# Decoder layer: the instruction order from a list scheduler with deadlines worked back from the matmuls, and the residual update on VectorE alone

## The chip, the cores and the metric

One core of a Trainium2 chip. The metric is the device time of one execution in microseconds; the kernel before took 1973.88 us (median of 3 runs, 1972.43 to 1973.93).

## What is computed

One layer of a decoder for 256 tokens and a width of 2048, in f32, with an RMS norm before and after each of four sub-layers:

```python
h = h + 0.5 * rmsnorm(swiglu(rmsnorm(h), ...))        # ff1: 2048 -> 2 x 5632 -> 2048
h = h + rmsnorm(mix(rmsnorm(h)))                       # one input projection; sparse attention (8 heads)
                                                       # beside a gated linear recurrence; one output projection
h = h + 0.5 * rmsnorm(swiglu(rmsnorm(h), ...))        # ff2
h = h + rmsnorm((p @ w_ple_proj) * sigmoid(rmsnorm(h) @ w_ple_gate))   # ple
```

## The kernel before, in words

**Matmuls.** Weights come as *items* of 256 x 512 (512 KB). There are 692 of them: ff1 264, mix 128, ff2 264, ple 36. An item is loaded by SP into one of four `raw` tiles, and split into a high and a low part in one of eight `ring` slots: ACT makes the high part, DVE the low part ("ring split" below means DVE's half; with a gain it is a SCALAR_TENSOR_TENSOR of 128x512, two per item). An item is then multiplied with both blocks of 128 tokens (tb = 0 and 1), six matmuls of 128x512 per block. Block 1 follows block 0 at a lag of 4 or 5 items (`LAG`). A group of items adds up in one PSUM bank: A_76, A_77, A_78, B_79, B_80, B_81; the banks T_82 and T_83 serve transposes and small matmuls. The moving operand is a ring slot, the stationary one a slice of `uT` (input of a phase, transposed, high and low), `hT` (hidden units of a feed-forward phase) or `oT`.

**Inside a feed-forward phase.** A chunk of 512 hidden units is a gate group (A) and an up group (B). ACT takes silu of the gate into `sg`, DVE multiplies it with the up group into `hid`, PE transposes hid in four pieces (`tr`), and ACT and DVE split the result into hT. The down-projection's groups (`ev_down`) are added into `y`, 512 columns at a time (c = 0 to 3).

**Between phases.** `after_y` squares y with a running sum on ACT and multiplies y by the gain `gpost` on POOL (into `tmp` for c = 3). At c = 3, `finish` makes the block's statistic (sum on DVE, root on ACT, reciprocal on DVE), and `new_h` updates the residual h for the four c. For c = 0 and 1 that is one instruction of DVE; for c = 2 and 3 it is two of POOL. Then `next_u` transposes each piece of h on PE and splits it into uT, ACT the high and DVE the low part. `square_u` squares h for the next phase's first norm. There are three such boundaries: ff1 to mix, mix to ff2, ff2 to ple. At the end of ple all four pieces are on DVE, and h goes out by SP.

**What sets the order.** Every engine runs its instructions in the order in which the program issues them. `Emitter` keeps a clock of its own: `charge_pe` moves it by a fixed cost per matmul, `charge` estimates when ACT, DVE and POOL finish. Work beside the stream is put in a heap with a time (`after`: estimated readiness plus a slack of 500 or 800 ns; `later`: a fixed delay) and issued when the clock has passed it. `run_ops` walks through the matmuls and emits splits up to 10 us (`LOOK`) ahead of it, and loads as far as the raw tiles allow. `Engine.__getattr__` is the helper through which every operation of ACT, DVE, POOL and PE goes (line 176, so nearly all rows have that line); it issues at once. Loads of the gains (`load_gpost`) and of h stand where the program calls them. Tables of ACT are loaded early at four places by hand.

Of the kernel before, what the change touches and what calls it, by code (L numbers as in the profile page):

```python
# [153 lines left out]

def _free(ap):
    n = 1
    for d in ap.shape[1:]:
        n *= d
    return n


class Engine:
# [4 lines left out]
    def __init__(self, em, key, engine):  # L167
        self.em, self.key, self.engine = em, key, engine

    def __getattr__(self, name):  # L170
        f = getattr(self.engine, name)
        if name == "dma_start":
            return f

        def call(out, *args, **kw):
            r = f(out, *args, **kw)  # L176
# [7 lines left out]
            else:  # L184
                n = max([_free(out)] + [_free(a) for a in args[:1] if hasattr(a, "shape")])
# [8 lines left out]
            return r  # L194
# [3 lines left out]
def _build(nc, tc, ctx, dr, out):  # L198
    em = Emitter()
    sy = nc.sync  # L200
    ac, ve, gp_, pe = (Engine(em, k, e) for k, e in (("A", nc.scalar), ("V", nc.vector), ("G", nc.gpsimd), ("P", nc.tensor)))
# [237 lines left out]
    def finish(phase_next, tb, half):  # L439

        rstd(st[:, SS + tb * 4:SS + tb * 4 + 4], 4, col(RPOST + tb), half)
        if phase_next is None:
            if tb == 0:
                nc.scalar.preload_act_table(AF.Sigmoid)
            for c in range(4):
                new_h(tb, c, True)
                sy.dma_start(out[tb, :, c * 512:(c + 1) * 512], h[:, tb, c * 512:(c + 1) * 512])
        else:
# [7 lines left out]
            ready = em.ready, em.last  # L456
            for c in range(4):
                em.ready, em.last = ready
# [5 lines left out]
    def after_y(tb, c, phase_next, half, gain):  # L464
# [8 lines left out]
        gp_.tensor_tensor(tmp[:, tb] if c == 3 else y[:, tb, cc], y[:, tb, cc], gpost[:, cc], ALU.mult)  # L473
        if c == 3:
            finish(phase_next, tb, half)

# [7 lines left out]
    def open_pool(name, old=None):  # L484
        if old is not None:
            pools.pop(old).close()
# [14 lines left out]
    def ffn(ph, phase_next, get):  # L501
# [21 lines left out]
        def ev_down(half, oc):  # L523
            def f(tb, ps):
# [3 lines left out]
                else:  # L528
                    if oc == 2 and tb == 0:
                        nc.scalar.preload_act_table(AF.Sqrt)  # L530
# [506 lines left out]
    def ple(get):  # L1037
# [8 lines left out]
        def ev_gate(c):  # L1046
            def f(tb, ps):
                sg = get("sg")[:, tb]
                ac.activation(sg, ps, AF.Sigmoid, scale=col(RPRE + tb))
                if c == 3:  # L1050
                    nc.scalar.preload_act_table(AF.Sqrt)
# [49 lines left out]
    nc.scalar.preload_act_table(AF.Silu)  # L1101
# [116 lines left out]
    em.drain()  # L1218
    for s in list(pools.values()):
# [56 lines left out]
```

## Time and profile before

| | |
|---|---|
| median of 3 runs | 1973.88 us |
| the profiled execution: its own time | 1972.35 us |
| its span, first to last instruction | 1970.5 us |
| mean granted TensorE clock | 0.996 |
| bytes moved | 372.86 MB, mean 189 GB/s |

Times in rows are us from the span's start. PE is TensorE's matmul, PEld its weight load, DVE VectorE, ACT ScalarE, POOL GpSimd, SP SyncE, which issues the DMAs. A row names the tile written, `<-`, and the tiles read, and then the shapes. In a list by time, what stands in brackets at the end of a row is how long the engine had been idle before, and what ended that. A clock of 1.00 is full speed; PE has the levels 1.2 and 2.4 GHz. "x4" behind a row is a count of like instructions in a row.

### The profile page before, as it was taken

The page shows a single profiled execution, that of the slowest core. Times are in us where ns is not written, and L with a number is a line of the kernel's source. Part 1 is how long each engine was busy: PE and PEld are TensorE (multiplying, and loading weights), DVE is VectorE, ACT ScalarE, POOL GpSimd, SP SyncE. Part 2 cuts the span into 40 slices and gives each one's busy share as a digit, 9 for nine tenths or more (in the row PEclk, how much of TensorE's full clock was granted, in tenths as well). Part 3 has the DMA queues.
Part 4 walks back from the last instruction along what each step waited for, and adds up shares of the span by engine and source line. Part 5 has one row for each costly group of instructions (what it writes and reads, how often), then busy time and mean ns, then how long its engine had stood idle before and what let it go on. Part 6 is the DMA issues. An engine that isn't in the chain of part 4 may idle for free.

```text
span 1970.5 us, 24737 instructions
## 1 busy us (share of the span) xinstructions
PE 1941.5 (99%) x8896; PEld 1605.3 (81%) x8896; DVE 1143.8 (58%) x1597; ACT 1112.4 (56%) x1707; POOL 188.2 (10%) x225
## 2 busy tenths in 40 slices
PE   9999999999999999999999899999999999999998
PEld 7888888888888887888888688888888888888776
DVE  6655554455555557766767755555444555554665
ACT  7655544455554446766797665555444555544564
POOL 3000010000000013103511400000000000000301
PEclk9999999999999999999999999999999999999999
DMA  8755565565565655762446455555555556556463
GB/s 285 267 182 184 179 199 191 190 197 191 186 192 185 190 171 178 251 225 73 154 160 222 150 199 195 189 192 183 191 192 193 191 183 196 188 185 195 157 221 118
DMA packets 107850, 372.86 MB, mean 189 GB/s; under 512 B 11856, under 2 KB 19024, under 8 KB 106960
## 3 DMA queue, kind: packets, MB, share of 16 engines
q1 hardware_dynamic: 107584, 371.19, 57.5%
q8 instruction: 69, 1.13, 0.2%
q14 instruction: 53, 0.43, 0.1%
q10 hardware_dynamic: 144, 0.11, 0.0%
HBM read 369.15 MB, written 2.10 MB: 188 GB/s over the span
## 4 chain that ended last, share of the span: by engine, by line
PE 93%; DVE 3%; ACT 1%; issue 1%; DMA 0%; POOL 0%; SPq 0%; DVEq 0%; ACTq 0%; POOLq 0%
PE A L176 63%; PE B L176 29%; PE T L176 2%; DVE ring L176 2%; DVE uT L176 0%; DVE y L176 0%; ACT junk L176 0%; DVE h L176 0%; ACT ring L176 0%; ACT y L176 0%; DMA raw<-ff_w_gate 0%; POOL rt L176 0%; DVE st L176 0%; ACT st L176 0%; DVE sm L176 0%
## 5 line engine op out<-in xcount | busy, mean ns | idle before, releaser
L176 DVE SCALAR_TENSOR_TENSOR ring<-raw,vec,ring 128x512 fp32r<-128x512 f32 (+3 forms) x992 | 716.8, 765 | 388.1 <-ACT ring L176 386.2
L176 PE MATMUL A<-ring,uT 128*128 128x512 f32 (+3 forms) x3552 | 859.6, 389 | 9.4 <-DVE ring L176 3.5
L176 ACT ACTIVATE ring<-raw,vec 128x512 fp32r<-128x512 f32 (+3 forms) x992 | 669.8, 713 | 297.2 <-PE A L176 151.4
L176 PEld LDWEIGHTS A<-ring,uT 128*128 128x128 f32 x3552 | 654.1, 188 | 143.7 <-DVE ring L176 6.7
L176 PE MATMUL B<-ring,uT 128*128 128x512 f32 x2208 | 541.2, 389 | 0.0
L176 PE MATMUL A<-ring,hT 128*128 128x512 f32 x2112 | 490.6, 392 | 0.0
L176 PEld LDWEIGHTS B<-ring,uT 128*128 128x128 f32 x2208 | 414.1, 188 | 86.2
L176 PEld LDWEIGHTS A<-ring,hT 128*128 128x128 f32 x2112 | 396.2, 188 | 86.2
L176 DVE TENSOR_TENSOR ring<-raw,ring 128x1024 fp32r<-128x1024 f32 x196 | 242.7, 1241 | 255.7 <-ACT ring L176 255.6
L176 ACT ACTIVATE ring<-raw 128x1024 fp32r<-128x1024 f32 x196 | 207.3, 1058 | 240.1 <-PE A L176 190.0
L176 POOL TENSOR_TENSOR y<-y,gpost 128x512 f32<-128x512 f32 x24 | 31.1, 1297 | 1277.2 <-ACT junk L176 1277.2
L176 ACT ACTIVATE hT<-T 128x512 fp32r<-128x512 f32 x44 | 26.2, 598 | 95.9 <-PE T L176 95.9
L176 ACT ACTIVATE sg<-A,st 128x512 f32<-128x512 f32 x52 | 35.8, 688 | 72.7 <-PE A L176 72.6
L176 DVE TENSOR_TENSOR hT<-T,hT 128x512 fp32r<-128x512 f32 x44 | 30.3, 691 | 73.1 <-ACT hT L176 72.6
L176 ACT ACTIVATE junk<-y 128x512 f32<-128x512 f32 x31 | 19.6, 632 | 58.0 <-DVE y L176 58.0
L176 DVE SCALAR_TENSOR_TENSOR hid<-B,st,sg 128x512 f32<-128x512 f32 x44 | 32.8, 748 | 23.8 <-PE B L176 23.8
L176 PE MATMUL B<-ring,oT 128*64 128x256 f32 (+1 forms) x224 | 42.0, 327 | 0.0
L176 PEld LDWEIGHTS B<-ring,oT 128*64 128x64 f32 (+1 forms) x224 | 33.4, 157 | 5.4
L176 POOL TENSOR_TENSOR per_sc<-per_sc 128x32 f32<-128x32 f32 (+1 forms) x24 | 9.3, 388 | 193.9 <-ACT per_sc L176 188.9
L176 PEld LDWEIGHTS T<-cst,hid 128*128 128x128 f32 x176 | 21.9, 140 | 5.6
L176 PE MATMUL T<-cst,hid 128*128 128x128 f32 x176 | 26.2, 272 | 0.0
L176 ACT ACT_TABLE_LOAD x20 | 25.7, 1283 | 0.4
(157 smaller groups left out, 671.7 us busy)
## 6 DMA issues: line engine op xcount, KB each, us to landing
raw<-ff_w_up SPq DMA_DIRECT2D x176, 512.0 KB, 4.2
raw<-ff_w_down SPq DMA_DIRECT2D x176, 512.0 KB, 3.3
raw<-ff_w_gate SPq DMA_DIRECT2D x175, 512.0 KB, 4.1
raw<-w_out SPq DMA_DIRECT2D x32, 512.0 KB, 4.4
raw<-w_ple_gate SPq DMA_DIRECT2D x32, 512.0 KB, 4.3
raw<-cmp_w SPq DMA_DIRECT2D x16, 512.0 KB, 4.6
raw<-w_in_q SPq DMA_DIRECT2D x16, 512.0 KB, 4.6
raw<-w_in_y SPq DMA_DIRECT2D x16, 512.0 KB, 4.3
```

The costliest lines, as they stand in the source:

```text
L176: r = f(out, *args, **kw)
```

## The change

Every operation, and every DMA of SP, now goes into a list (`Plan.add`) with the blocks of memory that it reads and writes, and estimates of how long it holds its engine (`step`) and when its result is there (`lat`). `Plan.flush` (called when a pool of tiles is opened, three times, and at the end) finds the dependences, gives each matmul a due time by its place in the stream (transposes and small matmuls 2 us earlier, `AUX`), works due times back through the dependences, and then places the operations one at a time: the engine that can start first takes, of what is ready, what is due first. A load isn't placed more than 15 us ahead of its due time (`AHEAD`). DVE and POOL exclude each other in it where both use the port (`port`). In the order of the planned starts, the operations are then issued. Table loads are put ahead of the first operation of a new set (`SETS`), in place of the four by hand.

Beside that, `new_h` is one instruction of DVE for every c, and the multiplication by gpost for c = 3 is DVE's too. The Emitter's heap stays and sets the order in which the list is recorded.

```diff
+class Plan:
...
+    HOP, SAME, PE_MARGIN, NEAR, AUX, AHEAD = 60.0, 35.0, 150.0, 120.0, 2000.0, 15000.0
...
+            if name == "scalar_tensor_tensor":
+                s = 132.0 + 1.04 * n
+            elif name in ("tensor_scalar", "tensor_copy") and len(sbuf) == 1:
+                s = 135.0 + 0.53 * n
+            else:
+                s = 65.0 + 1.045 * n
...
+            two = len(sbuf) >= 2 or name in ("tensor_scalar", "tensor_copy")
+            return s, s + 85.0, two and n > 32
...
+    def flush(self):
...
+        t = max(self.nominal, self.free["P"])
+        for o in ops:
+            if o["key"] == "P":
+                o["due"] = t - (self.AUX if o["aux"] else 0.0)
+                t += o["step"]
+            else:
+                o["due"] = None
+        self.nominal = t
+        for i in range(len(ops) - 1, -1, -1):
+            o = ops[i]
+            due = o["due"] if o["due"] is not None else t
+            for j in o["succ"]:
+                q = ops[j]
+                raw = q["deps"][i]
+                if q["key"] == o["key"]:
+                    d = o["lat"] + self.SAME if raw and o["key"] in "AVG" else o["step"]
+                else:
+                    d = o["lat"] + self.HOP
+                if o["key"] == "S":
+                    d = 2300.0 + o["bytes"] / 250.0
+                due = min(due, q["due"] - d)
+            o["due"] = due
+
+        left = [len(o["deps"]) for o in ops]
...
+        at = [max(o["floor"], o["due"] - self.AHEAD if o["key"] == "S" else 0.0) for o in ops]
...
+        while len(order) < n:
+            best = None
+            for k, c in ready.items():
+                if not c:
+                    continue
+                f = self.free[k]
+                t0 = min(max(f, at[i]) for i in c)
+                if best is None or t0 < best[0]:
+                    best = (t0, k)
+            t0, k = best
+            c = ready[k]
+            i = min((i for i in c if at[i] <= t0 + self.NEAR), key=lambda i: (ops[i]["due"], i))
+            c.remove(i)
+            o = ops[i]
+            s = max(t0, at[i])
+            if o["port"]:
+                s = max(s, self.port["G" if k == "V" else "V"])
+                self.port[k] = s + o["lat"] - 30.0
+            start[i] = o["start"] = s
+            self.free[k] = s + o["step"]
+            end = s + o["lat"]
+            if k == "S":
+                self.dma = max(s + 2000.0, self.dma) + o["bytes"] / 310.0
+                end = self.dma + 300.0
+            order.append(i)
+            o["end"] = end
...
+            for j in o["succ"]:
+                q = ops[j]
+                raw = q["deps"][i]
+                if q["key"] == k and k != "S":
+                    r = end + self.SAME if raw and k in "AVG" else s + 1.0
+                else:
+                    r = end + self.HOP + (self.PE_MARGIN if q["aux"] else 0.0)
+                at[j] = max(at[j], r)
+                left[j] -= 1
+                if not left[j]:
+                    ready[q["key"]].append(j)
+        for i in sorted(range(n), key=lambda i: (start[i], i)):
+            ops[i]["fn"]() if ops[i]["fn"] else ops[i]["load"]["preload"]()
...
         def call(out, *args, **kw):
-            r = f(out, *args, **kw)
+            n = max([_free(out)] + [_free(a) for a in args[:1] if hasattr(a, "shape")])
+            self.plan.add(self.key, name, lambda: f(out, *args, **kw), out, args, kw, n)
+            if name == "activation":
+                func = args[1]
+                self.plan.ops[-1]["preload"] = lambda: self.engine.preload_act_table(func)
+            if self.key == "S":
+                return
...
-    def new_h(tb, c, last=False):
+    def new_h(tb, c):
         cc = slice(c * 512, (c + 1) * 512)
         a, hh = tmp[:, tb] if c == 3 else y[:, tb, cc], h[:, tb, cc]
-        if c < 2 or last:
-            ve.scalar_tensor_tensor(hh, a, col(RPOST + tb), hh, op0=ALU.mult, op1=ALU.add)
-        else:
-            gp_.tensor_scalar(a, a, col(RPOST + tb), None, op0=ALU.mult)
-            gp_.tensor_tensor(hh, a, hh, ALU.add)
+        ve.scalar_tensor_tensor(hh, a, col(RPOST + tb), hh, op0=ALU.mult, op1=ALU.add)
 
...
         if phase_next is None:
-            if tb == 0:
-                nc.scalar.preload_act_table(AF.Sigmoid)
             for c in range(4):
-                new_h(tb, c, True)
+                new_h(tb, c)
                 sy.dma_start(out[tb, :, c * 512:(c + 1) * 512], h[:, tb, c * 512:(c + 1) * 512])
...
         else:
             ac.activation(junk, y[:, tb, cc], AF.Square, accum_out=col(SS + tb * 4 + c))
-        gp_.tensor_tensor(tmp[:, tb] if c == 3 else y[:, tb, cc], y[:, tb, cc], gpost[:, cc], ALU.mult)
         if c == 3:
+            ready = em.ready, em.last
+            ve.tensor_tensor(tmp[:, tb], y[:, tb, cc], gpost[:, cc], ALU.mult)
+            em.ready, em.last = ready
             finish(phase_next, tb, half)
+        else:
+            gp_.tensor_tensor(y[:, tb, cc], y[:, tb, cc], gpost[:, cc], ALU.mult)
...
     def open_pool(name, old=None):
+        plan.flush()
```

What the new order does at three places (of each program the rows as they stand, the older one first). `h` is the residual, `y` and `tmp` the output of a phase, `st` the statistic, `ring<-raw,vec,ring` a ring split.

**PE, boundary ff1 to mix.** Transposes of h (`<-cst,h`) stand among the last matmuls of ff1 (`hT`) and the first of mix (`uT`).

```order
L176 MATMUL A_77<-ring,hT 128x512 x24
L176 MATMUL T_83<-cst,h 128x128 x4
L176 MATMUL T_82<-cst,h 128x128 x4
L176 MATMUL A_77<-ring,hT 128x512 x12
L176 MATMUL B_79<-cst,h 128x128 x4
L176 MATMUL A_78<-ring,uT 128x512 x12
L176 MATMUL B_81<-cst,h 128x128 x4
L176 MATMUL A_78<-ring,uT 128x512 x6
L176 MATMUL T_83<-cst,h 128x128 x4
L176 MATMUL A_78<-ring,uT 128x512 x6
L176 MATMUL T_82<-cst,h 128x128 x4
L176 MATMUL B_79<-cst,h 128x128 x4
```

```order
L419 MATMUL A_77<-ring,hT 128x512 x21
L419 MATMUL T_83<-cst,h 128x128 x4
L419 MATMUL A_77<-ring,hT 128x512
L419 MATMUL T_82<-cst,h 128x128 x4
L419 MATMUL A_77<-ring,hT 128x512
L419 MATMUL B_79<-cst,h 128x128 x4
L419 MATMUL A_77<-ring,hT 128x512
L419 MATMUL B_81<-cst,h 128x128 x4
L419 MATMUL A_77<-ring,hT 128x512 x12
L419 MATMUL A_78<-ring,uT 128x512 x22
L419 MATMUL T_83<-cst,h 128x128 x4
L419 MATMUL A_78<-ring,uT 128x512
```

Block 0's four transposes of h were in three places, with 12 matmuls between the second and the third, and 12 and 6 of the new phase after them; they now follow 21 matmuls instead of 24, with one matmul between. Block 1's come after 22 matmuls of the new phase.

**DVE, the same boundary**, from the last y of block 0 (`y<-A_76`).

```order
L176 TENSOR_TENSOR y<-A_76,y 128x512
L176 TENSOR_REDUCE st<-st 128x1
L176 RECIPROCAL st<-st 128x1
L176 SCALAR_TENSOR_TENSOR h<-y,st,h 128x512 x2
L176 SCALAR_TENSOR_TENSOR ring<-raw,vec,ring 128x512 x4
L176 TENSOR_TENSOR uT<-T_83,uT 128x4x128
L176 TENSOR_TENSOR uT<-T_82,uT 128x4x128
L176 TENSOR_TENSOR y<-A_77,y 128x512
```

```order
L419 TENSOR_TENSOR y<-A_76,y 128x512
L419 TENSOR_TENSOR tmp<-y,gpost 128x512
L419 SCALAR_TENSOR_TENSOR ring<-raw,vec,ring 128x512
L419 TENSOR_REDUCE st<-st 128x1
L419 SCALAR_TENSOR_TENSOR ring<-raw,vec,ring 128x512 x2
L419 RECIPROCAL st<-st 128x1
L419 SCALAR_TENSOR_TENSOR h<-y,st,h 128x512 x3
L419 SCALAR_TENSOR_TENSOR h<-tmp,st,h 128x512
L419 TENSOR_TENSOR uT<-T_83,uT 128x4x128
L419 TENSOR_TENSOR uT<-T_82,uT 128x4x128
L419 SCALAR_TENSOR_TENSOR ring<-raw,vec,ring 128x512 x2
L419 TENSOR_TENSOR uT<-B_79,uT 128x4x128
```

Two pieces of h were followed by four ring splits; now four pieces of h come in a row, with the multiplication for tmp and three ring splits ahead of the reciprocal.

**DVE, the end of the kernel**, from the reciprocal of block 0.

```order
L176 RECIPROCAL st<-st 128x1
L176 SCALAR_TENSOR_TENSOR h<-y,st,h 128x512 x3
L176 SCALAR_TENSOR_TENSOR h<-tmp,st,h 128x512
L176 TENSOR_TENSOR y<-sg,B_81 128x512
L176 SCALAR_TENSOR_TENSOR junk,st<-y 128x512
L176 TENSOR_REDUCE st<-st 128x1
L176 RECIPROCAL st<-st 128x1
L176 SCALAR_TENSOR_TENSOR h<-y,st,h 128x512 x3
L176 SCALAR_TENSOR_TENSOR h<-tmp,st,h 128x512
```

```order
L419 RECIPROCAL st<-st 128x1
L419 SCALAR_TENSOR_TENSOR h<-y,st,h 128x512 x3
L419 TENSOR_TENSOR y<-sg,B_81 128x512
L419 SCALAR_TENSOR_TENSOR junk,st<-y 128x512
L419 TENSOR_REDUCE st<-st 128x1
L419 TENSOR_TENSOR tmp<-y,gpost 128x512
L419 RECIPROCAL st<-st 128x1
L419 SCALAR_TENSOR_TENSOR h<-tmp,st,h 128x512
L419 SCALAR_TENSOR_TENSOR h<-y,st,h 128x512 x3
L419 SCALAR_TENSOR_TENSOR h<-tmp,st,h 128x512
```

tmp's multiplication now stands between the sum and the reciprocal, and the last piece of block 0 (`h<-tmp`) behind block 1's reciprocal. Before that end, on PE, the last run of matmuls of block 1 alone (A_76) has 18 instead of 36.

**PE, a chunk of ff1**, from the last items of block 0's up group (B_80) to the transposes of its hid.

```order
L176 MATMUL B_80<-ring,uT 128x512 x6
L176 MATMUL B_81<-ring,uT 128x512 x6
L176 MATMUL B_80<-ring,uT 128x512 x6
L176 MATMUL B_81<-ring,uT 128x512 x6
L176 MATMUL A_76<-ring,hT 128x512 x6
L176 MATMUL T_83<-cst,hid 128x128 x4
L176 MATMUL B_81<-ring,uT 128x512 x6
```

```order
L419 MATMUL B_80<-ring,uT 128x512 x6
L419 MATMUL B_81<-ring,uT 128x512 x5
L419 MATMUL B_80<-ring,uT 128x512
L419 MATMUL B_81<-ring,uT 128x512
L419 MATMUL B_80<-ring,uT 128x512 x5
L419 MATMUL B_81<-ring,uT 128x512 x5
L419 MATMUL T_83<-cst,hid 128x128 x4
L419 MATMUL B_81<-ring,uT 128x512
L419 MATMUL A_76<-ring,hT 128x512 x6
```

The transposes stood behind 12 matmuls after the last of B_80, and now stand behind 5.

On SP, the loads of h (two, 1 MB each) and of ff1's gpost moved from the early up and gate items of ff1 to the last down items: gpost after the 37th of 40, h after the 38th and after mix's first item. At the start, both halves of the first gate item now precede the first piece of x, and the first up item precedes the second piece.

## Rows read from the trace of the kernel before

**Rows 1.** The page: busy time of each engine, share of the span, instructions.

```profile
PE 1941.5 (99%) x8896; PEld 1605.3 (81%) x8896; DVE 1143.8 (58%) x1597; ACT 1112.4 (56%) x1707; POOL 188.2 (10%) x225
```

**Rows 2.** Busy time by stretch: stretch, its length, PE, PEld, DVE, ACT, POOL, clock, DMA.

```profile
60.00:285.00 225.00, 225.00 (x1010) 186.15 (x1009) 127.63 (x177) 122.97 (x181) 10.02 (x30) 1.00 0.62 206
735.00:760.00 25.00, 21.16 (x100) 16.59 (x99) 22.16 (x30) 17.13 (x38) 17.77 (x11) 0.93 0.44 148
760.00:1050.00 290.00, 286.56 (x1515) 242.49 (x1514) 197.12 (x381) 217.62 (x412) 73.56 (x101) 1.00 0.54 173
1105.00:1131.00 26.00, 19.43 (x91) 14.95 (x90) 21.36 (x32) 16.47 (x36) 17.43 (x11) 0.93 0.38 118
1850.00:1882.00 32.00, 29.05 (x139) 22.70 (x138) 26.80 (x38) 23.88 (x49) 14.49 (x9) 1.00 0.51 167
1882.00:1971.00 89.00, 79.34 (x350) 65.34 (x348) 50.99 (x72) 46.27 (x73) 11.28 (x8) 0.96 0.48 159
```

**Rows 3.** Timeline of the first boundary (DVE, POOL, PE) and the second (PE, from 1126.99).

```profile
731.92 0.69 DVE L176 TENSOR_TENSOR y<-A,y 128x512 f32<-128x512 f32 x1 [2.59 <-PE A L176]
...
736.02 2.44 DVE L176 SCALAR_TENSOR_TENSOR ring<-raw,vec,ring 128x512 fp32r<-128x512 f32 x2
...
734.32 2.12 POOL L176 TENSOR_SCALAR y<-y,st 128x512 f32<-128x512 f32 x1 [0.33 <-DVE st L176]
736.52 1.38 POOL L176 TENSOR_TENSOR h<-y,h 128x512 f32<-128x512 f32 x1
737.89 2.01 POOL L176 TENSOR_SCALAR tmp<-tmp,st 128x512 f32<-128x512 f32 x1
739.98 1.38 POOL L176 TENSOR_TENSOR h<-tmp,h 128x512 f32<-128x512 f32 x1
...
737.22 1.04 PE L176 MATMUL T<-cst,h 128*128 128x128 f32 x8
...
755.03 2.01 PE L176 MATMUL A<-ring,uT 128*128 128x512 f32 x4 [2.66 <-DVE uT L176]
756.83 1.06 PE L176 MATMUL B<-cst,h 128*128 128x128 f32 x4
...
1126.99 0.92 PE L176 MATMUL A<-cst,h 128*128 128x128 f32 x4 [4.51 <-DVE uT L176]
1127.57 2.91 PE L176 MATMUL A<-ring,uT 128*128 128x512 f32 x6
```

**Rows 4.** DVE's ring splits by form: from 734 to 752, then from 290 to 420.

```profile
L176 DVE SCALAR_TENSOR_TENSOR ring<-raw,vec,ring 128x512 fp32r<-128x512 f32 x10 | 10.7, 1130 | 0.0
...
L176 DVE SCALAR_TENSOR_TENSOR ring<-raw,vec,ring 128x512 fp32r<-128x512 f32 x18 | 12.9, 751 | 10.9 <-ACT ring L176 10.8
```

**Rows 5.** Timeline inside ff1: DVE's splits and hid, then PE.

```profile
221.18 1.43 DVE L176 SCALAR_TENSOR_TENSOR ring<-raw,vec,ring 128x512 fp32r<-128x512 f32 x2 [1.29 <-ACT ring L176]
222.52 0.75 DVE L176 SCALAR_TENSOR_TENSOR hid<-B,st,sg 128x512 f32<-128x512 f32 x1
...
223.62 1.52 PE L176 MATMUL A<-ring,uT 128*128 128x512 f32 x6
...
226.35 0.60 PE L176 MATMUL T<-cst,hid 128*128 128x128 f32 x4
```

**Rows 6.** Timeline of the end: the last matmuls, block 1's evacuation and its pieces of h.

```profile
1946.22 15.12 PE L176 MATMUL A<-ring,uT 128*128 128x512 f32 x66
...
1961.44 0.69 ACT L176 ACTIVATE sg<-A,st 128x512 f32<-128x512 f32 x1 [4.25 <-PE A L176]
...
1964.33 2.23 DVE L176 SCALAR_TENSOR_TENSOR h<-y,st,h 128x512 f32<-128x512 f32 x3
1966.49 0.74 DVE L176 SCALAR_TENSOR_TENSOR h<-tmp,st,h 128x512 f32<-128x512 f32 x1
```

**Rows 7.** Loads of gpost, from issue to landing; and the page's rate in 40 slices.

```profile
DMA to landing us min/median/max: 7.2/7.6/7.9
...
GB/s 285 267 182 184 179 199 191 190 197 191 186 192 185 190 171 178 251 225 73 154 160 222 150 199 195 189 192 183 191 192 193 191 183 196 188 185 195 157 221 118
```

More of the change, by code (lines that the diff above doesn't have):

```diff
@@ L165, with __init__ @@
     RATE = {"A": (100.0, 0.84), "V": (70.0, 1.04), "G": (80.0, 2.2)}
-    def __init__(self, em, key, engine):
-        self.em, self.key, self.engine = em, key, engine
+    def __init__(self, em, plan, key, engine):
+        self.em, self.plan, self.key, self.engine = em, plan, key, engine
     def __getattr__(self, name):
         f = getattr(self.engine, name)
-        if name == "dma_start":
+        if name == "dma_start" and self.key != "S":
             return f
         def call(out, *args, **kw):
-            r = f(out, *args, **kw)
+            n = max([_free(out)] + [_free(a) for a in args[:1] if hasattr(a, "shape")])
[5 more added lines that the diff above has]
+                return
             if self.key == "P":
@@ L184, in call @@
             else:
-                n = max([_free(out)] + [_free(a) for a in args[:1] if hasattr(a, "shape")])
                 a, b = self.RATE[self.key]
@@ L193, in call @@
                 self.em.charge(self.key, a + b * n + (90.0 if kw.get("accum_out") is not None else 0.0))
-            return r
         return call
@@ L199, in _build @@
     em = Emitter()
-    sy = nc.sync
-    ac, ve, gp_, pe = (Engine(em, k, e) for k, e in (("A", nc.scalar), ("V", nc.vector), ("G", nc.gpsimd), ("P", nc.tensor)))
+    plan = Plan()
+    ac, ve, gp_, pe, sy = (Engine(em, plan, k, e) for k, e in (
+        ("A", nc.scalar), ("V", nc.vector), ("G", nc.gpsimd), ("P", nc.tensor), ("S", nc.sync)))
     PS = bass.MemoryType.PSUM
@@ L455, in finish @@
                     held.setdefault(id(b), []).append(uflag(phase_next, t, c))
-            ready = em.ready, em.last
             for c in range(4):
-                em.ready, em.last = ready
                 new_h(tb, c)
@@ L472, in after_y @@
             ac.activation(junk, y[:, tb, cc], AF.Square, accum_out=col(SS + tb * 4 + c))
-        gp_.tensor_tensor(tmp[:, tb] if c == 3 else y[:, tb, cc], y[:, tb, cc], gpost[:, cc], ALU.mult)
         if c == 3:
+            ready = em.ready, em.last
+            ve.tensor_tensor(tmp[:, tb], y[:, tb, cc], gpost[:, cc], ALU.mult)
+            em.ready, em.last = ready
             finish(phase_next, tb, half)
+        else:
+            gp_.tensor_tensor(y[:, tb, cc], y[:, tb, cc], gpost[:, cc], ALU.mult)
     def load_gpost(name):
@@ L528, in f @@
                 else:
-                    if oc == 2 and tb == 0:
-                        nc.scalar.preload_act_table(AF.Sqrt)
                     ve.tensor_tensor(yy, ps, yy, ALU.add)
@@ L1100, in _build @@
         nc.tensor.matmul(bankT[0][:, :128], junk[:, :128], junk[:, :128], start=True, stop=True)
-    nc.scalar.preload_act_table(AF.Silu)
     xT = y.rearrange("p a b -> p (a b)").rearrange("p (k t) -> p k t", k=KT)
@@ L1218, in _build @@
     em.drain()
+    plan.flush()
     for s in list(pools.values()):
```

147 lines of the change are left out of this document (145 added, 2 removed).

## The prediction

> **What bounds the kernel now.** I read the totals of the page first: TensorE (PE) is busy for 1941.5 of a span of 1970.5 us, VectorE (DVE) for 58% and ScalarE (ACT) for 56% [rows 1]. The matmul stream itself is the limit, and no edit here removes a matmul. What an order can win is only the 29.0 us in which PE stands still (1970.5 − 1941.5) and the time in which it runs slowly. So the second view is the busy time by stretch [rows 2]: look for stretches in which PE's busy time is less than the stretch, or the granted clock is under 1. Inside the feed-forward phases PE fills the stretch to the last digit (225.00 of 225.00). The idle time lies elsewhere: first phase boundary (ff1 to mix) 3.84; mix 3.44; second boundary (mix to ff2) 6.57; third (ff2 to ple) 2.95; last stretch 9.66; most of the rest is the start. The two largest boundaries also show a clock of 0.93.
>
> The third view, the timeline of the first boundary, says why PE waits there [rows 3]. The statistic of a token block needs the whole block, so each block goes through square, sum, root, reciprocal, residual update h, transposes, and the split into uT, before the next phase can read it. Two things stretch that chain. Half of each update is on POOL, at 2.12 + 1.38 + 2.01 + 1.38 us, one after the other [rows 3], while DVE makes a piece of h in 0.74 [rows 6]. And DVE's queue puts eight ring splits ahead of the uT splits that PE waits for: PE's 2.66 us wait at 755.03 ends on a uT. At the second boundary the same wait is 4.51 us [rows 3]. Behind both, PE runs at the lower of its two levels for a while: four 512-wide matmuls take 2.01 us, where six at full clock take 1.52 [rows 3, 5]. (From 1.52 for six and 15.12 for sixty-six [rows 5, 6]: 0.227 a matmul, and 0.39 from the start of the last to its end.)
>
> **POOL's work also slows DVE's.** Ten ring splits between 734 and 752 average 1.130 us, and the same form takes 0.751 in an undisturbed stretch [rows 4]. One pair shows it closely: two splits that start at 736.02 take 2.44 us, and POOL's h starts in the middle of them and runs to 737.90 [rows 3].
>
> The Trainium skill, "SBUF — State Buffer", section "Who interferes with whom", says that a VectorE instruction with two SBUF inputs and a GpSimd instruction that reads SBUF exclude each other for a whole instruction. By this rule the POOL work of a boundary (2 × (2.12 + 1.38 + 2.01 + 1.38) = 13.8 us) could hold up DVE for up to 13.8 us; the measured excess is what I count. The rule also speaks against the change, which makes DVE's side longer and leaves 24 multiplications on POOL; that is rival 2.
>
> **The change, part by part.** Twelve pieces of h move from POOL to DVE (c = 2 and 3, two blocks, three boundaries), with eight multiplications by gpost (c = 3). Per boundary DVE gains 4 × 0.74 of h [rows 6] and 2 multiplications at about 0.69 (nearest row: DVE's TENSOR_TENSOR of the same size, y<-A, 0.69 [rows 3]), 4.3 us, and loses what the disturbance cost the ring splits: 10 × (1.130 − 0.751) = 3.8 us [rows 4]. So DVE's load is about even, and the POOL chain of 6.9 us per block is gone.
>
> **First boundary, replayed by the new order** with durations of these rows; pieces that follow without a wait start 0.68 apart (two ring splits in 1.43 us, one in 0.75 [rows 5]). y of block 0 ends at 732.61. DVE: tmp to 733.3, one ring split to 734.0, sum to 734.15 (ACT's square of y is done by then: ACT is not behind a ring split here), two ring splits to 735.5, reciprocal 735.7, h at 736.4, 737.1, 737.8, 738.5. PE: the order has 21 matmuls instead of 24 ahead of the transposes, so they start at 737.22 − 3 × 0.227 = 736.54, then 737.2, 737.85, 738.5 with one matmul between. Each finds its piece ready. Then 12 matmuls to 741.7 and 22 of the new phase to 746.7. Block 1: y waits for four uT and two ring splits and ends at 743.2; sum 744.7, two ring splits 746.1, reciprocal 746.25, h 747.0. The transpose waits 0.35 us. The uT are then ahead of their readers by 1 us or more. Left over: about 0.5.
>
> **Second boundary.** By the same steps (evacuation, tmp, another group's y, sum, two ring splits, reciprocal) the first h is ready 0.9 + 3.9 = 4.8 us after block 0's last matmul, and in the order PE has 29 matmuls in between, 6.6 us. POOL's multiplication of the last c = 2 piece falls into DVE's ring splits there and can hold one up for its whole length, about 1.4 as for POOL's other products [rows 3]; the 1.8 us of slack hold that. For block 1 DVE makes four h, five ring splits and two uT in a row; PE comes about 0.3 us too early for block 1's first uT, 0.35 for the next, and the two roots on ACT may add 0.8. Left over: about 1.5. **Third:** one ring split fewer ahead of the reciprocal and six more matmuls (pT) for block 1; left over 0.3.
>
> The loss at the three boundaries is 3.84 + 6.57 + 2.95 = 13.4 us idle [rows 2], and about 3.1 of slow clock: against 0.227 a matmul and 0.60 for four transposes [rows 5], the first boundary loses 0.9 + 0.5 and the second 0.3 + 1.4 [rows 3]. The left-over waits are under 1 us each, far from the 2.66 behind which the clock fell, so I count no slow clock. 16.5 − 2.3 = **14.2 us gained**, bounds 8 (chain half repaired) and 16.5 (all).
>
> **Loads.** The order defers h's two loads (1 MB each) and gpost (1 MB) from the early weights to the last items of ff1's second down-projection, on SP's one queue ahead of the next phase's raw tiles. A 1 MB gpost takes 7.2 to 7.9 us to land, and the first two slices of the page carried 285 and 267 GB/s [rows 7]. From about 704 us the queue then has 6.5 MB up to the fourth tile of the mix phase: at 267 GB/s some 25 us, landed by 731, first needed by DVE at about 733 to 746. Nothing on the path, with 2 us to spare at the tightest.
>
> **Mix.** 3.44 us of waits [rows 2]. I did not replay the attention's many short operations; between 0 (new waits for old) and 3.4 gained I take 1.5, with 3 lost as the low end.
>
> **Start.** Both halves of the first weight tile now precede x, and the first up tile precedes x's second piece. The same bytes must land before the stream is dense; PE's first matmul comes later, the dense stream not. No row shows the new order, so 0, with 1 us either way.
>
> **Steady transposes.** PE now does a block's four transposes of hid 5 matmuls behind the block's last one, before it was 12; today they stand 3.1 us behind hid's end (226.35 against 222.52 + 0.75 [rows 5]). The last matmul of a group ends 0.39 after its start, an evacuation starts 0.10 after that (1961.44 against 1961.34 [rows 6]) and hid takes 0.75: 1.24, against 6 × 0.227 = 1.36. 0.12 us of slack is kept by the order; if hid stands behind one ring split (0.68), the transposes wait 0.56. 44 such groups: between 0 and 25 us. The ring splits themselves follow PE, so their place is stable; I take 1.0 lost.
>
> **End.** Now h ends 5.9 us after the last matmul (1967.23 − 1961.34) [rows 6]. Three edits lengthen that. tmp's multiplication is on DVE between sum and reciprocal beside ACT's root, which covers about half of it: +0.3. The last piece of block 0 stands ahead of block 1's pieces: +0.7. And block 0's last matmul comes 18, not 36, ahead of block 1's, 4.1 us; its chain up to its third piece takes about 5.5, so block 1's y starts 0.6 late; less what POOL's tmp costs h today (0.1): **1.5 lost**, bounds 0.3 and 2.5.
>
> **Sum**, against the profiled execution (1972.35 us, 1.85 of it around the span): −14.2 − 1.5 + 0 + 1.0 + 1.5 = −13.2, 1959.2. The median of the runs, 1973.88, is 1.5 above it, so I forecast **1960.5**.
>
> **Rivals.** (1) *Half the gain.* The reciprocal still stands behind two ring splits on DVE, and if a raw tile or ACT's half of a split is late, everything in that queue is late: h slips by the same time and the clock falls again. Against it: the tiles land earlier by the replay. Gain 8 − 4 = 4 to 8: 1966 to 1970. Chance 0.14.
> (2) *POOL and DVE exclude each other where the plan did not place them.* Multiplications of y now start when gpost has landed, in a burst before a boundary and before the end; each can hold up a DVE split for 1 us (the 2.44 us pair against 1.43 [rows 3, 5]). Two on each block's chain cost 2 × 2 × 3 × 1.0 = 12 at the three boundaries, of which slack takes about half: 1967. Chance 0.06; it needs gpost to land within about 10 us of the boundary. By the rule of the Trainium skill quoted above the exclusion lasts a whole instruction; the pair in the trace agrees.
> (3) *Slower.* The 44 transposes come too early: from a mean wait of 13.2/44 = 0.3 us beyond what I count, the gain is gone, and at 0.56 the kernel is at about 1984. For it: slack of 0.12. Against: DVE is busy for 127.63 of 225 us of such a stretch [rows 2], so that hid finds it free about every other time. Chance 0.07.
> (4) *No change*: the new order merely moves the waits. Against: the four POOL steps on the chain are gone whatever the order. Chance 0.05.
> Forecast: 0.68.
>
> **How the numbers follow.** A measurement can tell 0.2%, 3.9 us. Faster takes the forecast, (1) but for its upper end, and (2): 0.87. Same: (4) and that end, 0.07. Slower: 0.06. Low end, all of the boundaries (16.5), mix 3.4, start 1, end 0.3 lost: 1953. High end, with the half gain taken in: 1969.
>
> **What would show it.** Right: PE fills 735 to 760 and the two other boundaries but for 1 us each, with the clock at 1; POOL's rows h<-y, h<-tmp and TENSOR_SCALAR y are gone; DVE's ring splits there take 0.75; h ends some 7.4 us after the last matmul. Wrong: waits of PE on hid's transposes, a DMA as what ends ACT's ring waits at a boundary, or a clock under 1 there.

## The result and the profile after

The changed kernel takes **1951.22 us** (median of 4 runs, 1949.27 to 1953.99) against 1973.19 before: ratio 0.989, 95% interval 0.9873 to 0.9907, so 18 to 25 us less. The direction was forecast; the gain was 22 us where I had 13.4, and the time lies 1.8 us under the low end of my range.

The page of the changed kernel, busy time by engine ([rows 1] before):

```profile
span 1947.9 us, 24736 instructions
PE 1934.3 (99%) x8896; PEld 1602.0 (82%) x8896; DVE 1149.6 (59%) x1617; ACT 1125.9 (58%) x1706; POOL 148.3 (8%) x193
```

The matmuls are the same 8896, yet PE's *busy* time fell by 7.2 us. Its idle time fell from 29.0 to 13.6. Busy time by stretch of the changed kernel: the three boundaries, mix, the end ([rows 2] before; stretches of the same lengths, but for the end, which was 89 us):

```profile
735.00:760.00 25.00, 25.00 (x128) 21.00 (x127) 23.40 (x41) 22.39 (x48) 4.08 (x4) 1.00 0.61 190
1092.00:1118.00 26.00, 26.00 (x132) 21.56 (x131) 23.98 (x41) 21.84 (x49) 1.89 (x2) 1.00 0.42 136
1831.00:1863.00 32.00, 32.00 (x159) 26.83 (x158) 26.98 (x46) 26.56 (x53) 0.00 (x0) 1.00 0.57 171
760.00:1050.00 290.00, 289.45 (x1529) 243.95 (x1528) 199.42 (x384) 220.95 (x412) 81.34 (x101) 1.00 0.57 178
1865.00:1948.00 83.00, 72.90 (x322) 60.00 (x320) 47.02 (x67) 42.25 (x64) 9.40 (x6) 0.97 0.50 160
```

Read the counts in brackets behind PE. The three boundary stretches now hold 128, 132 and 159 matmuls; before, 100, 91 and 139 [rows 2]. Each holds the same 32 transposes of h, so 89 wide matmuls (of 512 columns) more fit in the same time: 89 x 0.227 = 20.2 us. The idle time there was only 13.4. That difference is where my sum went wrong.

The first boundary of the changed kernel, PE, DVE and ACT ([rows 3] before):

```profile
732.60 0.74 DVE L419 SCALAR_TENSOR_TENSOR ring<-raw,vec,ring 128x512 fp32r<-128x512 f32 x1
...
733.33 1.40 DVE L419 SCALAR_TENSOR_TENSOR ring<-raw,vec,ring 128x512 fp32r<-128x512 f32 x2
...
734.90 2.08 DVE L419 SCALAR_TENSOR_TENSOR h<-y,st,h 128x512 f32<-128x512 f32 x3
735.88 0.60 PE L419 MATMUL T<-cst,h 128*128 128x128 f32 x4
736.23 0.48 PE L419 MATMUL A<-ring,hT 128*128 128x512 f32 x1
736.55 0.60 PE L419 MATMUL T<-cst,h 128*128 128x128 f32 x4
...
744.92 2.08 DVE L419 SCALAR_TENSOR_TENSOR h<-y,st,h 128x512 f32<-128x512 f32 x3
...
746.09 0.60 PE L419 MATMUL T<-cst,h 128*128 128x128 f32 x4
746.44 0.48 PE L419 MATMUL A<-ring,uT 128*128 128x512 f32 x1
...
748.46 8.89 PE L419 MATMUL A<-ring,uT 128*128 128x512 f32 x38
```

Every transpose finds its piece of h and every matmul its uT: no bracket with a wait stands behind any PE row. DVE's ring splits take 0.74 and 0.70 where ten averaged 1.13 [rows 4]. From the first of four transposes over the one matmul behind them to the next transpose it is 736.55 − 735.88 = 0.67, so a transpose costs (0.67 − 0.227)/4 = 0.11.

With 0.227 and 0.11 the loss of any stretch can be counted, whatever the rows overlap: from the start of its first matmul to the start of its last, less what the matmuls between need. **By this count the boundaries lost 6.5, 9.5 and 4.6 us before, 20.6 in all, and 0.15, 0.4 and 0.2 now.** Where a stretch is cut moves the count of a boundary by some 0.2 us, in the runs below at times by 0.5. I use the sum of the three below as "boundary loss".

### The profile page after: what moved, and what is told of

Its sections match the earlier page's. It is cut to its first block, busy times and chain, and to the rows that moved or that the text cites. A ratio compares the mean times of both kernels' runs of the same rounds, so it can differ in the third digit from the quotient of the medians.

```text
span 1947.9 us, 24736 instructions
## 1 busy us (share of the span) xinstructions
PE 1934.3 (99%) x8896; PEld 1602.0 (82%) x8896; DVE 1149.6 (59%) x1617; ACT 1125.9 (58%) x1706; POOL 148.3 (8%) x193
## 3 DMA queue, kind: packets, MB, share of 16 engines
q8 instruction: 69, 1.13, 0.2%
## 4 chain that ended last, share of the span: by engine, by line
PE 99%; DVE 0%; DMA 0%; POOL 0%; ACT 0%; SPq 0%; issue 0%; DVEq 0%; POOLq 0%
PE A L419 66%; PE B L419 30%; PE T L419 2%; DMA raw<-ff_w_up 0%; DVE h L419 0%; POOL rt L419 0%; DVE junk L419 0%; DVE y L419 0%; SPq L419 0%; DVE tmp L419 0%; POOL zt L419 0%; ACT ring L419 0%; ACT sg L419 0%; DVEq L1512 0%; DVE st L419 0%
## 5 line engine op out<-in xcount | busy, mean ns | idle before, releaser
L419 ACT ACTIVATE ring<-raw,vec 128x512 fp32r<-128x512 f32 (+3 forms) x992 | 684.9, 718 | 427.6 <-PE A L419 243.5
L419 PE MATMUL A<-ring,uT 128*128 128x512 f32 (+3 forms) x3552 | 883.8, 390 | 1.6 <-ACT uT L419 1.6
L419 POOL TENSOR_TENSOR y<-y,gpost 128x512 f32<-128x512 f32 x24 | 41.0, 1739 | 1308.4 <-DMA gpost<-ff_post_g 1158.0
L419 ACT ACTIVATE sg<-A,st 128x512 f32<-128x512 f32 x52 | 35.4, 681 | 19.9 <-PE A L419 19.9
L419 DVE TENSOR_TENSOR hT<-T,hT 128x512 fp32r<-128x512 f32 x44 | 30.3, 691 | 14.2 <-ACT hT L419 11.9
L419 POOL TENSOR_SCALAR junk<-xT,vec 128x256 f32<-128x256 f32 x24 | 29.0, 1207 | 61.9 <-ACT xT L419 37.3
L419 PE MATMUL A<-ring,oT 128*128 128x512 f32 x96 | 25.5, 397 | 0.0
```

Of the source, the lines that this page charges most:

```text
L419: self.plan.add(self.key, name, lambda: f(out, *args, **kw), out, args, kw, n)
```

## Experiments

**1. Which half of the change?** The control first, then each half alone. `dve_only` is the old program with

```diff
-        if c < 2 or last:
-            ve.scalar_tensor_tensor(hh, a, col(RPOST + tb), hh, ...)
-        else:
-            gp_.tensor_scalar(a, a, col(RPOST + tb), None, op0=ALU.mult)
-            gp_.tensor_tensor(hh, a, hh, ALU.add)
+        ve.scalar_tensor_tensor(hh, a, col(RPOST + tb), hh, ...)
```

and the c = 3 multiplication on VectorE; `plan_pool` is the changed program with these edits reversed.

> The changed kernel once more, as the control on the same chip as the next three. Both theories: 1949 to 1954, and again PE fills every stretch but the start, about 0.6 us at 780 to 800, and the end.

> The hand-written order with the residual update and the c = 3 multiplication on VectorE, no list scheduler. Theory 'POOL': the chain of four POOL steps and the hold-up of DVE by them make the loss at the boundaries, so most of the 22.7 us comes without the scheduler: 1953 to 1958. Theory 'order': in the hand order eight ring splits still stand ahead of block 1's uT splits, and its transposes now wait for all four h, so waits of 1 to 4 us stay at the boundaries, the clock falls behind them, and only 3 to 10 us are gained: 1963 to 1970.

> The list scheduler with the residual update of c = 2 and 3 and the c = 3 multiplication back on POOL; it knows POOL's durations and puts matmuls of the next phase between the transposes. Theory 'POOL': the chain of 6.9 us a block cannot be covered and DVE is held up where POOL works: 1962 to 1970, waits of over 2 us at the two large boundaries. Theory 'order': the scheduler covers most of it, 1952 to 1958, waits under 1 us each.

| | median us | ratio, 95% interval | boundary loss us |
|---|---|---|---|
| before | 1973.40 | | 20.6 |
| dve_only | 1967.72 | 0.9962 to 0.9985 | 13.3 |
| plan_pool | 1955.15 | 0.9892 to 0.9925 | 5.4 |
| both (after_again) | 1949.85 | 0.9868 to 0.9898 | (after) 0.7 |

The scheduler alone gives 18 us, the residual update alone 6, both 23.5: they add up. "Order" holds by its times, "POOL" falls. But "order" had waits under 1 us each, and POOL's chain is what the scheduler can't quite cover: one wait for POOL's h lasts 1.4. PE's waits in plan_pool from 700 to 1900 (engine, what it waited for, us in all, times, longest):

```profile
PE B L419 <- POOL h L419: 2.1, 3, 1.4
PE A L419 <- POOL h L419: 0.8, 2, 0.5
```

In dve_only the waits are long, and behind VectorE and ScalarE. Its timeline at the first boundary:

```profile
751.05 1.04 PE L176 MATMUL B<-cst,h 128*128 128x128 f32 x8
...
753.58 0.29 ACT L176 ACTIVATE st<-st,cst 128x1 f32<-128x1 f32 x1 [0.72 <-DVE st L176]
753.78 1.32 ACT L176 ACTIVATE ring<-raw,vec 128x512 fp32r<-128x512 f32 x2
...
755.01 1.06 ACT L176 ACTIVATE uT<-T 128x512 fp32r<-128x512 f32 x2
755.63 0.73 PE L176 MATMUL A<-ring,uT 128*128 128x512 f32 x2 [2.16 <-ACT uT L176]
```

The transposes are done at 752.1; ACT's uT starts at 755.0, behind squares of h, the next norm's root and two ring splits. The root waits for DVE's sum, which stands behind ring splits too. Of the 16.9 us between the spans of dve_only (1964.8) and the changed kernel 12.6 lie at the boundaries, 2.9 in mix and 1.9 at the start, by the start of the same wide matmul in both; at the end dve_only is 0.5 ahead.

**2. Which queue?** In the changed program one engine at a time takes its instructions in the order in which the hand-written code records them; the scheduler places the others around it:

```diff
+        hand = [i for i, o in enumerate(ops) if o["key"] == "P"][::-1]     # "V", "A" for the other two
...
+                if k == "P":
+                    c = [i for i in hand[-1:] if i in c]
...
-            i = min((i for i in c if at[i] <= t0 + self.NEAR), key=lambda i: (ops[i]["due"], i))
+            i = hand.pop() if k == "P" else min(...)
```

> The changed kernel, but PE takes its instructions in the order in which the hand-written code records them (as in dve_only); all other engines stay with the list scheduler. Theory 'PE order' (the gain of the scheduler, 17 us beside dve_only, is made by where matmuls stand between the transposes): most of it is lost, 1961 to 1968. Theory 'other queues' (it is made by uT standing ahead of ring splits and of the squares of h on DVE and ACT): 1951 to 1957.

> The same with VectorE in the recorded order, PE and the others with the scheduler. If VectorE's queue (eight ring splits and y of the next block ahead of uT) is what held PE: 1957 to 1966. If it is PE's order or ACT's queue: 1950 to 1955.

> The same with ScalarE in the recorded order. In dve_only the first uT splits of block 1 start 2.9 us after the transposes are done, behind four squares of h, a root and ring splits on ScalarE. If that queue is the wait: 1956 to 1964. If PE's or VectorE's order is: 1950 to 1955.

Against 1972.94 before on this chip: strict_pe 1953.37, strict_dve 1965.14, strict_act 1962.10. Boundary loss 2.1, 7.8, 6.2. So the matmuls that the new order puts between the transposes are worth little; the order on DVE's and ACT's queues carries the boundaries. What the three cost does not add up to the scheduler's 18 us: 3.5, 15.3 and 12.2 are each the price of one hand order among four planned ones. strict_act shows the queue (first boundary; block 1's transposes of h are done at 753.8):

```profile
753.69 1.32 ACT L422 ACTIVATE ring<-raw,vec 128x512 fp32r<-128x512 f32 x2
...
756.41 0.63 ACT L422 ACTIVATE junk<-h 128x512 f32<-128x512 f32 x1
...
757.86 0.29 ACT L422 ACTIVATE st<-st,cst 128x1 f32<-128x1 f32 x1 [0.73 <-DVE st L422]
758.06 1.32 ACT L422 ACTIVATE ring<-raw,vec 128x512 fp32r<-128x512 f32 x2
...
758.80 1.42 DVE L422 SCALAR_TENSOR_TENSOR ring<-raw,vec,ring 128x512 fp32r<-128x512 f32 x2 [0.45 <-ACT ring L422]
...
759.29 1.06 ACT L422 ACTIVATE uT<-T 128x512 fp32r<-128x512 f32 x2
...
759.61 4.71 PE L422 MATMUL A<-ring,uT 128*128 128x512 f32 x19 [0.28 <-DVE ring L422]
```

The same queue as in dve_only: uT comes 5.5 us behind the transposes, after squares of h that are needed later. But PE waits for no uT in strict_act. Its waits at the boundaries all end on a split of weights, on ACT's half or DVE's: what hurts is that the same squares and the root also hold up ACT's half of a split (758.06), and DVE's half behind it. The visible ones are seven, of 0.12 to 0.28 us, 1.4 in all of a loss of 6.2. In strict_dve too the most of PE's waiting is for DVE's ring splits (6.1 us), with 1.3 for a piece of h. My prediction spoke of DVE's eight ring splits; of ACT it said only that the square of y is not held up and that two roots may add 0.8.

Not all of the two losses is at the boundaries: both kernels also lose 4 to 5 us up to the first down-projection, where PE waits once, 2.1 us for DVE's half of a split in strict_dve and 2.5 for ACT's half in strict_act, and runs at the lower clock behind it (granted clock 0.91 in 245 to 265 and in 230 to 250).

**3. The scheduler's model.** `no_port` drops the one rule that DVE and POOL exclude each other:

```diff
-            if o["port"]:
+            if False:
```

> The changed kernel with the one rule taken out by which the scheduler lets DVE and POOL exclude each other. Since hardly any POOL work is left near a boundary I expect no change, 1949 to 1953, with a wait under 1 us more where POOL multiplies y. If the rule carries the plan (POOL busy where DVE is due): 1954 to 1960.

1967.99 against 1972.94 (0.9964 to 0.9987): over 16 us of the gain gone, where I expected none; it is beyond the 1954 to 1960 of my second theory too. The boundary loss is 1.4; 14 of the 16.3 us by which the span grows go in mix. First PE's waits there (760 to 900), then the longest on the timeline:

```profile
PE T L419 <- POOL zt L419: 11.5, 6, 6.1
```

```profile
868.62 0.67 ACT L419 ACTIVATE zt<-A,st 128x512 f32<-128x512 f32 x1
...
871.57 1.03 POOL L419 TENSOR_TENSOR ar<-ar,junk 128x256 f32<-128x256 f32 x1
...
873.59 0.72 POOL L419 TENSOR_TENSOR ar<-ar,junk 128x256 f32<-128x256 f32 x1
...
875.97 1.00 POOL L419 TENSOR_TENSOR rt<-zt,cs 128x128 f32<-128x128 f32 x3
877.05 0.45 POOL L419 TENSOR_TENSOR zt<-rt 128x128 f32<-128x128 f32 x1
877.56 1.12 PE L419 MATMUL T<-cst,zt 128*128 128x128 f32 x4 [6.11 <-POOL zt L419]
```

zt is ready for POOL at 869.3, but POOL has a row of `ar` products ahead of it. In the changed kernel rt starts right behind zt (ends 862.82):

```profile
862.89 1.02 POOL L419 TENSOR_TENSOR rt<-zt,cs 128x128 f32<-128x128 f32 x3 [0.57 <-ACT zt L419]
```

Behind the wait of 6.11 us PE runs at the lower clock for a while (granted clock 0.93 in 850 to 900), which adds to the loss. That the rule is worth this much is shown; that a plan without it believes POOL faster than it is, and so puts filler where a deadline is near, is inferred, since the planned times are not in a trace. The Trainium skill, "SBUF — State Buffer", section "Who interferes with whom", gives the rule (whole-instruction exclusion of a two-input VectorE instruction and a GpSimd read). The trace of the kernel before agrees in part: of the pair of splits in [rows 3] the second takes 1.77 us instead of 0.74, over POOL's h of 1.38; but within POOL's TENSOR_SCALAR of 2.12 us a piece of h on DVE takes 1.18 instead of 0.75 and ends 0.34 before it. I had priced the exclusion only as a hold-up of DVE; here it mattered as a number inside the plan.

**4. What does a wait cost?** `early_hid` puts the transposes of hid right behind the start of hid in the plan:

```diff
+        for i, o in enumerate(ops):
+            if o["aux"] and any(b[0].startswith("hid") for b in o["reads"]):
+                start[i] = max(start[j] + 1.0 for j in o["deps"])
```

> The changed kernel, but in PE's order the 44 groups of transposes of hid stand 3 to 8 matmuls earlier, right behind the place where DVE begins hid in the plan. I estimate that each then waits 0.5 to 0.6 us for hid (it ends 0.18 us ahead of the transposes in 1 of 2 cases today, and lasts 0.75). Theory 'start': a wait costs the whole delay of PE's next start, 44 x 0.55 = 24 us, 1971 to 1980, while the idle time of PE grows by 0.16 less per wait (17 us), since the row of the matmul ahead runs on for 0.39 - 0.227 = 0.16 into the wait. Theory 'idle': the time grows by what the idle time grows, and both by under 18 us.

1984.45 against 1973.40 (1.0043 to 1.0073), 34.6 above the control. The waits were longer than my 0.55: in the trace the 44 steps ahead of these transposes take 41.9 us instead of 10.3, 0.72 more each. Its page, and from the rows on hid who waited for it:

```profile
PE 1945.4 (98%) x8896; PEld 1599.3 (81%) x8896; DVE 1149.7 (58%) x1617; ACT 1123.1 (57%) x1706; POOL 146.3 (7%) x193
...
PE T L422: 24.7, 44
```

31.6 us waited, 24.7 of them visible: each wait hides 0.16 of itself (44 x 0.16 = 7.0). And 11 us of *busy* time appear without one matmul more, these 7.0 among them. The gentler version, with a margin of −400 for all transposes and small matmuls and then for hid's alone:

```diff
-                    r = end + self.HOP + (self.PE_MARGIN if q["aux"] else 0.0)
+                    r = end + self.HOP + ((-400.0 if any(b[0].startswith("hid") for b in q["reads"]) else self.PE_MARGIN) if q["aux"] else 0.0)
```

> The changed kernel with PE_MARGIN at -400 instead of 150: the transposes of hid stand about 2 matmuls (0.45 us) earlier, and the other transposes and small matmuls too. About 30 of 44 groups, which have 0.18 us to spare today, then wait some 0.27 us. Theory 'start': 30 x 0.27 = 8 us and some more at the other transposes: 1958 to 1963, while PE's idle time grows by only 30 x (0.27 - 0.16) = 3 us. Theory 'idle': 1952 to 1955.

> The changed kernel with a margin of -400 instead of 150 for the transposes of hid alone (in hid_2_earlier the small matmuls of the mix phase were moved too, some of them ahead of the short operation that makes their input). In hid_2_earlier these transposes waited 0.10 us more each (13.17 against 10.32 us for the 44 steps ahead of them), and only 0.23 us of that showed as idle. Theory 'start': the feed-forward phases get 3 to 6 us longer, 1953 to 1957, and PE's idle time stays within 1 us of the changed kernel's. Theory 'idle': no idle time, no loss, 1949 to 1952.

hid_2_earlier: 1959.97 against 1974.02; in it three transposes of zt in the mix phase stand ahead of the POOL operation that makes their input, and read old data, so only its feed-forward phases are read. That its time falls into the range of "start" is luck: the 44 steps take 13.2 us, 0.07 more each on average and not 0.27 for thirty of them, and 5.1 of the 10.3 us that it is behind the changed kernel at the last matmul are lost at the first boundary and in mix. hid_only: 1954.41 against 1973.75 (0.9886 to 0.9919; the interval overlaps that of after_again, so the reading rests on the traces), and this is its page, then 220 us of ff2 in the changed kernel and in hid_only:

```profile
span 1952.1 us, 24735 instructions
PE 1939.1 (99%) x8896; PEld 1599.6 (82%) x8896; DVE 1150.5 (59%) x1617; ACT 1125.0 (58%) x1706; POOL 146.3 (7%) x193
```

```profile
1150.00:1370.00 220.00, 220.00 (x992) 182.05 (x991) 125.80 (x174) 122.03 (x174) 0.00 (x0) 1.00 0.58 189
```

```profile
1150.00:1370.00 220.00, 220.00 (x987) 180.55 (x986) 125.43 (x175) 121.68 (x175) 0.00 (x0) 1.00 0.57 188
```

The span is 4.2 us longer, the idle time 13.0 against 13.6: **the whole loss lies in time that counts as busy.** Both stretches are full to the last digit; only the count of matmuls differs. From the 250th to the 3050th wide matmul, all in ff1, hid_only takes 2.6 us more than the changed kernel, and from the 4450th to the 7250th, in ff2, 2.2 more, where after_again differs by 0.1 at most; 2.8 of these 4.8 us stand in the 44 steps ahead of the transposes, most of the rest between the four of a group. "Start" holds, "idle" falls.

**5. The start and the end.** `loads_early` sets `AHEAD` to 1e9; `best_tail` keeps the recorded order for PE's last 120 instructions and puts ple's c = 3 multiplication on POOL.

```diff
-    HOP, SAME, PE_MARGIN, NEAR, AUX, AHEAD = 60.0, 35.0, 150.0, 120.0, 2000.0, 15000.0
+    HOP, SAME, PE_MARGIN, NEAR, AUX, AHEAD = 60.0, 35.0, 150.0, 120.0, 2000.0, 1e9
```

```diff
+        tail = set(hand[:LAST]) if not keep else set()
...
+                    c = [i for i in c if i not in tail or i == hand[-1]]
...
-            ve.tensor_tensor(tmp[:, tb], y[:, tb, cc], gpost[:, cc], ALU.mult)
+            (gp_ if phase_next is None else ve).tensor_tensor(tmp[:, tb], y[:, tb, cc], gpost[:, cc], ALU.mult)
```

> The changed kernel with no limit on how early SP places a load (AHEAD). The loads of x, cst, gpost and h (over 4 MB) then stand ahead of the seventh weight tile. Theory 'deferral is worth nothing' (my prediction): 1949 to 1953. Theory 'the start is bound by bytes': gpost and h, 3 MB at 300 GB/s, delay the early weights by 10 us, of which the head start of four raw tiles covers little: 1956 to 1961, all of it in the first 40 us.

> The changed kernel, but the last 120 instructions of PE keep the recorded order (block 0's last matmul 36, not 18, ahead of block 1's), and in ple POOL multiplies y by gpost for c = 3. In strict_pe, which also ends with 36, h ended 5.9 us after the last matmul with that multiplication on VectorE, in the changed kernel 6.65. Theory 'run of 18': the end gets 0.8 us shorter by the order and nothing or 0.1 more by POOL: span 1947 to 1948, time 1949 to 1951, the same within what the runs can tell. Theory 'multiplication' (it costs 0.3 between sum and reciprocal): the end gets 1.1 us or more shorter than in the changed kernel.

loads_early: 1958.34 against 1974.02 (0.9911 to 0.9941), 8.5 behind the control; at the 500th wide matmul it is already 8.4 us late. From 20 to 40 us, in the changed kernel and in loads_early:

```profile
20.00:40.00 20.00, 20.00 (x90) 16.57 (x89) 18.31 (x29) 16.12 (x27) 0.00 (x0) 1.00 0.95 315
```

```profile
20.00:40.00 20.00, 15.41 (x63) 12.59 (x64) 14.19 (x24) 14.07 (x22) 11.67 (x29) 0.83 0.91 318
```

The queue moves as many bytes a second, but x, gpost and h ahead of the fifth weight tile (not the seventh, as I had written). That tile lands 10.7 us after its issue, PE waits 3.5 and 2.9 us, and the granted clock of the stretch is 0.83. "Bound by bytes" holds, and the theory that I had called my prediction falls: the limit on early loads is worth 8 us at the start, and nothing at the boundary that the loads were deferred to.

best_tail: 1949.01 against 1974.02 (0.9859 to 0.9892), no difference from the control that the runs can tell. The last matmul and the last pieces of h, in the changed kernel and in best_tail:

```profile
1933.66 4.24 PE L419 MATMUL A<-ring,uT 128*128 128x512 f32 x18
...
1938.96 0.68 DVE L419 TENSOR_TENSOR y<-sg,B 128x512 f32<-128x512 f32 x1
...
1943.80 0.75 DVE L419 SCALAR_TENSOR_TENSOR h<-tmp,st,h 128x512 f32<-128x512 f32 x1
```

```profile
1936.76 1.75 PE L427 MATMUL A<-ring,uT 128*128 128x512 f32 x7
...
1943.65 0.74 DVE L427 SCALAR_TENSOR_TENSOR h<-tmp,st,h 128x512 f32<-128x512 f32 x1
```

h ends 6.65 us behind the last matmul in the first, 5.88 in the second, 5.89 before. In the first, block 1's y starts 0.27 us after its `sg` (ends 1938.69), since DVE is still on block 0's h, whose last piece then stands ahead of block 1's. strict_pe also ends with 36 and has 5.88 with the multiplication still on VectorE: the 0.77 is the run of 18 alone, and where the multiplication stands makes no difference. best_tail is the version I would keep; in span it is 0.2 us shorter, since its stream ran 0.6 longer up to the last matmul.

## Why the prediction was right and wrong

| term of the sum, us | forecast | measured |
|---|---|---|
| boundaries | −14.2 | −19.9 (20.6 − 0.7) |
| mix | −1.5 | −2.9 (idle 3.44 to 0.55) |
| start | 0 | −0.6 (at the 500th wide matmul; +0.1 in after_again) |
| steady transposes | +1.0 | +0.2 (44 steps, 10.1 to 10.3) |
| end | +1.5 | +0.8 |
| sum | −13.2 | −22.4; span −22.6 |

**The step that failed** is "the loss at the three boundaries is 13.4 us idle and about 3.1 of slow clock", and with it the upper bound 16.5, which I called all of it. The loss was 20.6. A row of a wide matmul lasts 0.39, the next could start after 0.227; a wait therefore shows in the idle time only from its 0.16th us on. Start by start, the three stretches of the kernel before hold 13.4 us of visible idle time in 12 waits, 2.1 hidden under the rows ahead of these waits, 0.9 in the matmuls right behind them (behind a wide one the next starts after 0.34 and not 0.227), 3.4 at the lower clock (I had counted 3.1), 0.5 in waits too short to show, and 0.4 that the two rounded costs leave over. I had called 16.5 the upper bound, and it was 4.1 too low; with 20.6 in its place the low end of my range would have been about 1949, and the measured time inside. Experiment 4 shows the mechanism both ways. The count of matmuls stood in [rows 2] all along: 65 wide ones and 32 transposes from start to start in the first stretch need 18.3 of its 24.8 us.

The Trainium skill, "Perfetto Trace Analysis", section "Identifying the Most-Contended Engine", warns of this: matmul busy share does not tell how near a kernel is to its bound; it points to the share of weight loads. The trace agrees: PEld was 16.59 of 25 at the first boundary [rows 2] and is 21.00 now, a loss of 25 x (1 − 16.59/21.00) = 5.3 us, nearer to the 6.4 measured than the idle 3.84. The same for the three boundaries is 5.3 + 8.0 + 4.9 = 18.2, where 19.9 were gained and 13.4 were idle. In hid_only it too shows what PE's busy time does not (182.05 to 180.55).

**Boundaries, the replay.** Right in its steps: the first transposes came at 735.88 where I had 736.54, block 1's at 746.09 where I had 746.7, and the whole stream of this execution runs 0.65 earlier from the start on, so both places are right to 0.05. I let block 1's y wait behind ring splits and uT until 743.2; it ends at 741.97, also 0.6 earlier when the 0.65 is taken off. Left over: 0.7 instead of 2.3 us, 1.6 of the error; the other 4.1 is the step above. What I had not seen is that ACT's queue needed the same repair as DVE's (experiment 2).

**Mix.** I had taken 1.5 without a replay; 2.9 came. It is the scheduler's: by the start of the same wide matmuls plan_pool keeps it to 0.1, and dve_only has none of it. Which of its waits the plan removes, and how, no run takes apart.

**Start.** The 0.6 is within what two executions of the changed kernel differ by (0.7), so nothing clear of 0.

**Slow clock.** Granted clock 1.00 in all three stretches, as forecast.

**Loads.** Right that nothing of them reaches the path at the boundary. The limit that defers them is worth 8 us at the start (experiment 5), which I had not priced; the kernel before had these loads behind the first weights too, so it is no part of the gain.

**Steady transposes.** The 0.12 us of slack that I read from the order is what the trace has: 0.12 at least, 0.19 in the median. (The 3.1 before was one group; the median of the 44 is 1.8.) By the count of wide matmuls the feed-forward phases cost the same before and after, to 0.1 us. Rival 3, that they come too early, fell for this plan, and its price is about right: 44 waits of 0.72 cost early_hid 34.6 us, 0.79 each. That early_hid and the rival both come to 1984 is chance: the rival had shorter waits and a base 10 us higher.

**End.** The right sign; I charged the multiplication 0.3, which cost nothing.

**The sum.** 1959.2 and the 1.5 of the median make 1960.7; the 1960.5 that I wrote is 0.2 lower and changes nothing.

**Rivals 1, 2 and 4** did not come. For rival 2 the runs show why: the plan knows the exclusion, and without it 16 us go, nearly all in mix, not at the boundaries where I looked.

## What to carry to other kernels

Where a stream of matmuls is the bound, measure a stretch by how many matmuls it holds, not by PE's idle time: with the rows of this kernel waits under 0.16 us are wholly hidden in busy time, and longer ones lose 0.16 of themselves there. A chain between two phases is only as short as the worst queue on it; read the queue of every engine that touches the chain, not that of the engine named in the longest wait, and look what else work on that queue pushes back: in strict_act it is the splits of the weights. A planned order is worth what its durations are worth: here one missing rule on two engines took back three quarters of the gain.

## What the runs showed of the hardware

Many short waits left TensorE's clock alone: early_hid waits 44 times 0.72 us, its mean granted clock is 0.999. For a single wait of 2 to 3 us its length did not decide. Behind dve_only's wait of 2.16 us at the first boundary the granted clock stays at 1.00, and so it does behind a wait of 2.61 in no_port (760 to 800). Behind dve_only's wait of 2.52 at the second boundary the stretch has 0.93 (a mean over both levels, 1.2 and 2.4 GHz), and behind the 2.12 of strict_dve 0.91. dve_only at the first and second boundary, no_port:

```profile
735.00:760.00 25.00, 21.15 (x107) 16.95 (x106) 21.70 (x38) 19.55 (x43) 3.59 (x2) 1.00 0.44 148
1105.00:1131.00 26.00, 22.37 (x105) 17.69 (x104) 21.81 (x38) 18.61 (x42) 1.30 (x1) 0.93 0.37 114
760.00:800.00 40.00, 35.55 (x168) 28.55 (x166) 25.85 (x31) 24.18 (x36) 8.97 (x16) 1.00 0.60 197
```

So no slow clock at a boundary can be read from the wait alone: where it matters, take the granted clock of the stretch.
